# First modulation by column halves with its shift as a one-row product, and the last output block by halves, in an encoder block on one core

## The chip, the core and the metric

The kernel runs on one core of a Trainium2 chip: TensorE (PE) for products, VectorE (DVE) and ScalarE (ACT) for element work, GpSimd (POOL), and SyncE (SP), which issues most transfers. The metric is the device time of one execution in microseconds (us), lower being better; the median of 3 runs is given. One more execution was profiled, and all rows below come from it.

## The reference, cut to what matters

One encoder layer on x (512 tokens by 1024 features, float32) with six modulation vectors of 1024 values:

```
mod = silu(c) @ W_ada + b_ada                 # six pieces of 1024
shift1, scale1, gate1, shift2, scale2, gate2 = split(mod)
h  = rmsnorm(x, g_norm1) * (1 + scale1) + shift1
z  = h @ W_in                                 # q latent 256 | kv latent 128 | rope key 64 | u 512 | v 512
y  = concat(rmsnorm(attention), rmsnorm(gMLP)) @ W_o ;  x = x + gate1 * y
h2 = rmsnorm(x, g_norm2) * (1 + scale2) + shift2
x  = x + gate2 * peer(h2)                     # product-key retrieval over 16384 experts
out = rmsnorm(x, g_final)
```

## The kernel before

Tokens are four blocks of 128 (NB = 4), features eight chunks of 128 (KD = 8). A float32 product of accuracy is three products of split parts (high and low half of each operand): `mm3`, lines 82 to 84; `split_into` makes the parts, the high one on ACT (L77), the low one on DVE (L78).

**The start.** SP loads the first modulation's scale weights (wada, group 1, eight chunks of 128 rows by 1024 columns, 512 KB each), then x (four blocks of 512 KB), then the shift weights (group 0, eight chunks), then the first two weight slabs of the input projection (wl0, wl1). SP's transfers go round over eight lanes, so that each waits for the one eight before it. `mod_cols` forms a modulation vector so: DVE adds up the eight chunks, each scaled by one column of silu(c) (csil), into macc, 128 partitions by 1024 (L143, L149, L146); PE transposes macc in eight pieces (mcol, L159); DVE sums each piece over its columns (L161) and adds the bias (L162). `normed_T` squares the four blocks of x on ACT (sq_n, L183), forms one reciprocal root for all four (n_ms on DVE, L112; n_r on POOL, L114), scales x on DVE (L197), has PE transpose it (trx_n, L201), applies scale and shift (nt_n, "the affine", L189 on DVE, L187 on ACT) and splits the result into hT.

**The projection.** lat (four blocks, 384 columns) and krp (512 columns) are PE products of hT with wl0 and wl1. Then ACT squares lat (sql, sqk), DVE copies it out of PSUM (L320), rq and rkv are formed (L112, L114), DVE scales lat (L326, L327), the rope key is rotated (kr, kr_t, L294 to L296), PE transposes lat (trl, L331), and queries, keys and values follow. kr_sw, which kr_t reads, and the three trl tiles share two PSUM buffers (tag tr).

**Later modulations** (groups 2 to 5) load on POOL's queue, after a marker that POOL copies once the first shift is there (mark, L247), and DVE adds them up between other work. mod_row (L177) multiplies macc by a matrix of ones on PE in two halves of 512 columns, in plain float32.

**The end.** The last four expert tiles' products (held, TAIL = 4) are done block by block of 128 tokens, for each of them the four experts, for each expert both column halves. Then the output blocks (the gather block GB, 0, 1, 2): on DVE times gate2 (L943), plus x (L944); square on ACT (L945); times g_final on DVE (L946); the two sums added (L947); reciprocal root (L112, L114); scaled on ACT in two halves (L951) and stored by SP (L952).

Which instruction of an engine stands where is set by the scheduler of the framework from a model, not by program order; where a stretch is under a manual schedule, its engines keep the program's order.

## Time and profile before

| what | value |
|---|---|
| median of 3 runs | 1567.47 us (1567.18 to 1567.62) |
| profiled execution, its own time | 1570.06 us |
| its span | 1568.3 us |
| mean granted TensorE clock | 0.981 |
| PE, DVE, ACT, POOL busy | 95%, 79%, 41%, 25% of the span |

The profiled execution is 2.59 us above the median; 1.8 us of its time lie outside the span. Times in the rows are microseconds from the span's start. A row of the timeline has the start, the time until its last instruction's end, engine, line, operation, written tile and read tiles, shape, number of instructions, and in brackets how long the engine was idle before it and for whom it waited.

### The profile page before, as it was taken

The numbers are of one execution on the slowest core, as the hardware profiler recorded it, in microseconds if no ns is written. First come the engines' busy times: TensorE is split into PE (matmuls) and PEld (weight loads), VectorE is DVE, ScalarE is ACT, GpSimd is POOL, SyncE is SP. The second block draws the span as 40 slices with busy tenths as digits, with TensorE's granted clock in tenths as the row PEclk, the third lists the DMA queues.
The fourth block names the chain that finished last, engine by engine and source line by source line (L and its number), as shares of the span: only waits on it lengthen the run. The fifth ranks groups of instructions, "written<-read, shape, count | busy, mean of one in ns | idle before, by whom it ended". The sixth has DMA issues, their size and how long they took to land.

```text
span 1568.3 us, 21451 instructions
## 1 busy us (share of the span) xinstructions
PE 1492.6 (95%) x7675; PEld 1317.9 (84%) x7675; DVE 1240.9 (79%) x2388; ACT 636.6 (41%) x1092; POOL 397.1 (25%) x335
## 2 busy tenths in 40 slices
PE   2899999998979999999999999999999999999996
PEld 1765787887879999999999999999999999998884
DVE  6937865579989997987887878878888888886774
ACT  2533434432338997334333333333333333332343
POOL 1202100000000000002554444444544544542210
PEclk9899999999999999999999999999999999999998
DMA  9626334331325769666999999988999998987873
GB/s 366 232 79 223 130 132 148 112 104 48 101 94 159 237 211 300 218 224 220 354 351 319 321 330 328 326 318 318 336 330 314 326 325 315 333 287 230 256 237 121
DMA packets 147226, 380.71 MB, mean 243 GB/s; under 512 B 11184, under 2 KB 59840, under 8 KB 146864
## 3 DMA queue, kind: packets, MB, share of 16 engines
q1 hardware_dynamic: 103472, 221.02, 40.5%
q0 software_dynamic: 42352, 153.62, 28.7%
q10 hardware_dynamic: 1296, 4.72, 0.8%
q8 instruction: 60, 0.98, 0.2%
q14 instruction: 46, 0.38, 0.1%
HBM read 349.16 MB, written 30.15 MB: 242 GB/s over the span
## 4 chain that ended last, share of the span: by engine, by line
PE 86%; DVE 7%; DMA 3%; ACT 1%; issue 1%; POOL 0%; SPq 0%; ACTq 0%; POOLq 0%; DVEq 0%
PE out L83 11%; PE out L84 11%; PE out L82 11%; PE pa L82 11%; PE pa L84 11%; PE pa L83 11%; PE gg L770 5%; DMA wada<-w_ada 2%; PE q L82 1%; PE q L84 1%; PE q L83 1%; PE yo L82 1%; PE yo L84 1%; PE yo L83 1%; DVE macc L149 1%
## 5 line engine op out<-in xcount | busy, mean ns | idle before, releaser
L842 POOL DMA_INDIRECT gu<-peer_u,idx x128 | 181.3, 1417 | 653.6 <-DVE w17l L78 467.6
L842 POOL DMA_INDIRECT gv<-peer_v,idx x128 | 173.0, 1351 | 235.0 <-DVE accg L862 209.0
L850 DVE SCALAR_TENSOR_TENSOR scr<-gu,h2g 128x1024 bf16<-128x1024 f32 x128 | 156.5, 1222 | 24.1 <-DMA gu<-peer_u,idx 21.8
L862 DVE SCALAR_TENSOR_TENSOR accg<-gv,wg,accg 128x1024 f32<-128x1024 f32 x127 | 162.8, 1282 | 7.1 <-DMA gv<-peer_v,idx 4.6
L770 PE MATMUL gg<-o,o 128*128 128x128 f32 x768 | 96.0, 280 | 3.6 <-ACT o L764 2.0
L770 PEld LDWEIGHTS gg<-o,o 128*128 128x128 f32 x768 | 94.6, 196 | 4.1 <-ACT o L764 4.1
L908 DVE TENSOR_TENSOR a<-a,g 128x384 f32<-128x384 f32 x128 | 69.1, 550 | 6.4 <-DMA g<-gd 2.9
L764 ACT ACTIVATE o<-o1b,gT 128x128 f32<-128x128 bf16 x192 | 63.4, 405 | 13.8 <-DVE o1b L751 7.2
L518 ACT ACTIVATE a<-pa 128x384 f32<-128x384 f32 x128 | 61.7, 483 | 13.2 <-PE pa L84 13.2
L149 DVE SCALAR_TENSOR_TENSOR macc<-wada,csil,macc 128x1024 f32<-128x1024 f32 x40 | 51.2, 1280 | 9.5 <-DMA wada<-w_ada 9.1
L753 DVE TENSOR_TENSOR o<-iota_s,gT 128x1024 f32<-128x1024 f32 x48 | 58.4, 1216 | 0.3 <-PE gg L770 0.2
L757 DVE TENSOR_SCALAR o<-iota_s,gT 128x128 f32<-128x128 f32 x192 | 53.2, 339 | 0.0
L779 ACT COPY st<-gg 128x512 f32<-128x512 f32 x96 | 50.5, 581 | 0.0
L159 PE MATMUL mcol<-ident_s,macc 128*128 128x128 f32 x32 | 7.4, 391 | 26.6 <-DVE macc L146 23.1
L135 POOL DMA_DIRECT2D wada<-w_ada x32 | 17.1, 535 | 59.9 <-DVE macc L149 24.3
L159 PEld LDWEIGHTS mcol<-ident_s,macc 128*128 128x128 f32 x32 | 5.5, 201 | 28.3 <-DVE macc L146 17.9
L424 ACT ACTIVATE pe<-s,mx 128x512 f32<-128x512 f32 x16 | 11.0, 688 | 28.4 <-DVE mx L422 20.8
L684 PE MATMUL sc<-keys_s,qT 128*128 128x128 f32 x128 | 18.1, 284 | 2.8 <-ACT qT L681 2.8
L751 DVE TENSOR_TENSOR o1b<-erep,gB 128x512 bf16<-128x512 bf16 x48 | 20.0, 416 | 0.9 <-ACT gB L734 0.9
L684 PEld LDWEIGHTS sc<-keys_s,qT 128*128 128x128 f32 x128 | 15.6, 191 | 5.7 <-ACT qT L681 4.3
L531 DVE MAX8 v12d<-s 128x8 f32<-128x128 f32 x48 | 12.7, 280 | 9.4 <-ACT s L686 9.4
L431 PEld LDWEIGHTS o<-vv,pts 128*128 128x128 f32 x128 | 16.1, 192 | 2.3 <-DVE mx L422 0.8
(2789 smaller groups left out, 4952.2 us busy)
## 6 DMA issues: line engine op xcount, KB each, us to landing
gd<-st SPq DMA_DIRECT2D x12, 1984.0 KB, 7.9
g<-gd SPq DMA_DIRECT2D x31, 768.0 KB, 8.4
wada<-w_ada POOLq DMA_DIRECT2D x32, 512.0 KB, 4.7
wada<-w_ada SPq DMA_DIRECT2D x16, 512.0 KB, 10.1
x<-x SPq DMA_DIRECT2D x4, 512.0 KB, 12.4
x<-x ACTq DMA_DIRECT2D x4, 512.0 KB, 3.8
x2d<-x ACTq DMA_DIRECT2D x4, 512.0 KB, 2.8
gu<-peer_u,idx POOLq DMA_INDIRECT x128, 7.3
```

What stands on the lines that cost most here:

```text
L82: nc.tensor.matmul(o, lhsT=lh, rhs=rh, start=first, stop=False)
L83: nc.tensor.matmul(o, lhsT=lh, rhs=rl, start=False, stop=False)
L84: nc.tensor.matmul(o, lhsT=ll, rhs=rh, start=False, stop=last)
L149: nc.vector.scalar_tensor_tensor(acc, w, csil[:, c:c + 1], acc, op0=ALU.mult, op1=ALU.add)
L518: nc.scalar.activation(t, p[:, :TD], AF.Gelu)
L753: nc.vector.tensor_tensor(o2s[n], iota.unsqueeze(1).to_broadcast([P, UT, P]), tT[:, 1, t0:t0 + UT].unsqueeze(2).to_broadcast([P, UT, P]), ...
L764: nc.scalar.activation(o1s[n][:, i, :], e[:, :, i], AF.Copy, scale=tT[:, 2, t0 + i:t0 + i + 1])
L770: nc.tensor.matmul(pgs[n][i // 4][:, i % 4 * P:(i % 4 + 1) * P], lhsT=o2[:, i, :], rhs=o1[:, i, :], start=True, stop=True)
L842: nc.gpsimd.indirect_dma_start(out=g, out_offset=None, in_=src, in_offset=bass.IndirectOffsetOnAxis(ap=idx[:, s:s + 1], axis=0))
L850: nc.vector.scalar_tensor_tensor(scr, g, 1.0, st["h2g"], op0=ALU.mult, op1=ALU.mult, accum_out=actg[:, n:n + 1])
L862: nc.vector.scalar_tensor_tensor(accg, g, wg[:, s:s + 1], accg, op0=ALU.mult, op1=ALU.add)
L908: nc.vector.tensor_tensor(wv3, wv3, gt[:, :, e % GE, :], op=ALU.mult)
```

## The change

The first modulation's weights are loaded by column halves: each transfer is 256 rows by 512 columns (512 KB), four for a half of scale or shift. SP's order is now scale half 0, x, shift half 0, wl0, scale half 1, shift half 1, wl1, wv0, wv1, wuq, wukv. A scale half is added up on DVE as before, 512 wide (mh), and transposed in four pieces (msc). A shift half is made on PE: eight float32 products of one column of csil with 512 columns of weights, summed in one row of PSUM (msh, 1x512), copied by ACT (mshr), and turned into a column by four products of one column each (mshc); DVE adds the bias. Each block of x gets its own reciprocal root. `hT_half(0)` makes the first four chunks of hT from the first halves, and the second halves follow. The marker waits for the second shift half, and the transfers of perm, of the positions and of group 2 on POOL stand behind it or behind the four reciprocal roots.

At the end PE takes the last block's held products first for column half 0, then for half 1. `output` multiplies only half 0 by g_final ahead of the sum of squares (yg); half 1 is one DVE operation with the root and g_final; half 0 is scaled on ACT and stored by ACT's queue. The output blocks 0, 1 and 2 stand under a manual schedule for DVE and ACT.

```diff
+        def mod_half_load(g, hf):
+            ws = []
+            for k in range(4):
+                w = M0.tile([P, 2, 512], F32, name=f"wada{g}_{hf}_{k}", tag="wada0", bufs=12)
+                nc.sync.dma_start(w, a["w_ada"][k * 256:(k + 1) * 256, g * D + hf * 512:g * D + (hf + 1) * 512]
+                                  .rearrange("(c p) n -> p c n", p=P))
+                ws += [w[:, 0, :], w[:, 1, :]]
+            return ws
+        def scale_half(hf, ws):
+            acc = M0.tile([P, 512], F32, name=f"mh{hf}", tag="mh", bufs=2)
+            nc.vector.tensor_scalar_mul(acc, ws[0], csil[:, 0:1])
+            for c in range(1, KD):
+                nc.vector.scalar_tensor_tensor(acc, ws[c], csil[:, c:c + 1], acc, op0=ALU.mult, op1=ALU.add)
+            p = ps.tile([P, 512], F32, name=f"msc{hf}", tag="mod" if hf else "oacc", bufs=1)
+            for j in range(4):
+                nc.tensor.transpose(p[:, j * P:(j + 1) * P], acc[:, j * P:(j + 1) * P], ident)
+            m = cp.tile([P, 4], F32, name=f"msc_{hf}")
+            nc.vector.reduce_sum(m, p.rearrange("p (j k) -> p j k", k=P), axis=AX.X)
+            nc.vector.tensor_add(m, m, bada[:, KD + hf * 4:KD + hf * 4 + 4])
+            nc.vector.scalar_tensor_tensor(m, m, 1.0, g1c[:, hf * 4:hf * 4 + 4], op0=ALU.add, op1=ALU.mult)
+            return m
+        def shift_half(hf, ws):
+            p = ps.tile([P, 512], F32, name=f"msh{hf}", tag="mod", bufs=1)
+            for c in range(KD):
+                nc.tensor.matmul(p[0:1, :], lhsT=csil[:, c:c + 1], rhs=ws[c], start=c == 0, stop=c == KD - 1)
+            row = M0.tile([1, 512], F32, name=f"mshr{hf}", tag="mshr", bufs=2)
+            nc.scalar.copy(row, p[0:1, :])
+            p = ps.tile([P, 512], F32, name=f"mshc{hf}", tag="mod", bufs=1)
+            for j in range(4):
+                nc.tensor.matmul(p[:, j:j + 1], lhsT=row[:, j * P:(j + 1) * P], rhs=ones[0:1, 0:1],
+                                 start=True, stop=True)
+            m = cp.tile([P, 4], F32, name=f"msh_{hf}")
+            nc.vector.tensor_add(m, p[:, :4], bada[:, hf * 4:hf * 4 + 4])
             return m
...
-        ws1 = [mod_load(1, c) for c in range(KD)]
+        wsc, wsh = [None] * 2, [None] * 2
+        wsc[0] = mod_half_load(1, 0)
         xs = []
         for b in range(NB):
             t = B.tile([P, D], F32, name=f"x{b}", tag=f"y{b}")
             nc.sync.dma_start(t, a["x"][b * P:(b + 1) * P, :])
             xs.append(t)
-        ws0 = [mod_load(0, c) for c in range(KD)]
-        s1 = mod_scale(1, g1c, ws1)
-        sh1 = mod_cols(0, ws0)
+        wsh[0] = mod_half_load(0, 0)
+        s1 = [scale_half(0, wsc[0])]
+        ss1 = cp.tile([P, NB], F32, name="ss1")
+        for b in range(NB):
+            sumsq(xs[b], ss1[:, b:b + 1], f"sq_n{b}")
+            r = rstd_of(ss1[:, b:b + 1], D, f"n{b}")
+            nc.vector.tensor_scalar_mul(xs[b], xs[b], r)
+        sh1 = [shift_half(0, wsh[0])]
+        hT = [B.tile([P, KD, T], F32R, name=f"hT{i}", tag=f"hT{i}") for i in range(2)]
+
+        def hT_half(hf):
+            for j in range(4 * hf, 4 * hf + 4):
+                p = (tr_ps if hf else acc_ps)(f"trx{j}")
+                for b in range(NB):
+                    nc.tensor.transpose(p[:, b * P:(b + 1) * P], xs[b][:, j * P:(j + 1) * P], ident)
+                t = B.tile([P, T], F32, name=f"nt{j}", tag="nt", bufs=2)
+                affine(j, t, p, s1[hf], sh1[hf], j % 4)
+                split_into(hT[0][:, j, :], hT[1][:, j, :], t)
+
+        hT_half(0)
+        wl = load_w("wl", a["w_in"], 0, 512, (0,))
+        wsc[1] = mod_half_load(1, 1)
+        wsh[1] = mod_half_load(0, 1)
+        wl += load_w("wl", a["w_in"], 0, 512, (1,))
+        s1.append(scale_half(1, wsc[1]))
+        sh1.append(shift_half(1, wsh[1]))
         mark = cp.tile([P, 1], F32, name="mark")
-        mark = nc.gpsimd.tensor_copy(mark, sh1[:, 0:1])
-        hT = [B.tile([P, KD, T], F32R, name=f"hT{i}", tag=f"hT{i}") for i in range(2)]
-        normed_T(xs, s1, sh1, hT[0], hT[1], "n1")
+        mark = nc.gpsimd.tensor_copy(mark, sh1[1][:, 0:1])
+        hT_half(1)
...
-            wl = load_w("wl", a["w_in"], 0, 512)
             nc.sync.dma_start(wuq, a["w_uq"].rearrange("(c p) n -> p c n", p=P))
             nc.sync.dma_start(wukv, a["w_ukv"])
...
-                for e_, wh, wl, vh, vl in held:
-                    for hf in range(2):
-                        sl = slice(hf * 512, (hf + 1) * 512)
-                        mm3(outs[2 * b + hf], (wh[:, bs], wl[:, bs]), (vh[:, sl], vl[:, sl]),
-                            e_ == 0, e_ == NE - 1)
+                steps = [(hf, h) for h in held for hf in range(2)]
+                if b == ND - 1:
+                    steps.sort(key=lambda s: s[0])
+                for hf, (e_, wh, wl, vh, vl) in steps:
+                    sl = slice(hf * 512, (hf + 1) * 512)
+                    mm3(outs[2 * b + hf], (wh[:, bs], wl[:, bs]), (vh[:, sl], vl[:, sl]),
+                        e_ == 0, e_ == NE - 1)
             held.clear()
...
-    for b in (GB, 0, 1, 2):
+    halves = [slice(hf * 512, (hf + 1) * 512) for hf in range(2)]
+
+    def output(b):
...
         ss = gp.tile([P, 2], F32, name=f"ssf{b}", tag="ssf", bufs=2)
-        for hf in range(2):
-            sl = slice(hf * 512, (hf + 1) * 512)
+        yg = gp.tile([P, 512], F32, name=f"yg{b}", tag="yg", bufs=2)
+        for hf, sl in enumerate(halves):
             nc.vector.tensor_mul(y[:, sl], accg[:, sl] if b == GB else outs[2 * b + hf], gate2[:, sl])
             nc.vector.tensor_add(y[:, sl], y[:, sl], xr[:, sl])
             nc.scalar.activation(xr[:, sl], y[:, sl], AF.Square, accum_out=ss[:, hf:hf + 1])
-            nc.vector.tensor_mul(y[:, sl], y[:, sl], gfin[:, sl])
+            if hf == 0:
+                nc.vector.tensor_mul(yg, y[:, sl], gfin[:, sl])
         nc.vector.tensor_add(ss[:, 0:1], ss[:, 0:1], ss[:, 1:2])
         r = rstd_of(ss[:, 0:1], D, f"fin{b}")
-        for hf in range(2):
-            sl = slice(hf * 512, (hf + 1) * 512)
-            nc.scalar.activation(y[:, sl], y[:, sl], AF.Copy, scale=r[:, 0:1])
-            nc.sync.dma_start(out[b * P:(b + 1) * P, sl], y[:, sl])
+        nc.scalar.activation(yg, yg, AF.Copy, scale=r[:, 0:1])
+        nc.vector.scalar_tensor_tensor(y[:, halves[1]], y[:, halves[1]], r[:, 0:1], gfin[:, halves[1]],
+                                       op0=ALU.mult, op1=ALU.mult)
+        nc.scalar.dma_start(out[b * P:(b + 1) * P, halves[0]], yg)
+        nc.sync.dma_start(out[b * P:(b + 1) * P, halves[1]], y[:, halves[1]])
+
+    output(GB)
+    with tc.manual_schedule(engines={nc.vector.engine, nc.scalar.engine}):
+        for b in range(ND):
+            output(b)
```

Three places in the orders of the engines, before and after. In the names, a number behind a tile tells one buffer from another.

PE at the start, before: the last transposes of x (x_122 is its fourth block), the shift's transposes (mcol), and the first product of the projection.

```order
L201 MATMUL trx_n_246<-ident_s,x_122 128x128
L201 MATMUL trx_n_255<-ident_s,x_122 128x128
L159 MATMUL mcol_0_176<-ident_s,macc_165 128x128 x4
L159 MATMUL mcol_1_182<-ident_s,macc_165 128x128 x4
L201 MATMUL trx_n_264<-ident_s,x_116 128x128
L201 MATMUL trx_n_264<-ident_s,x_118 128x128
L201 MATMUL trx_n_264<-ident_s,x_120 128x128
L201 MATMUL trx_n_264<-ident_s,x_122 128x128
L82 MATMUL krp<-hT_191,wl0h 128x512
```

PE at the same place after: the first shift half stands between the transposes of the third block of x (x_112) and the fourth (x_114).

```order
L271 MATMUL trx_293<-ident_s,x_112 128x128
L271 MATMUL trx_302<-ident_s,x_112 128x128
L188 MATMUL msh_171<-wada_0_0_116,csil 1x512 x2
L188 MATMUL msh_171<-wada_0_1_118,csil 1x512 x2
L188 MATMUL msh_171<-wada_0_2_120,csil 1x512 x2
L188 MATMUL msh_171<-wada_0_3_122,csil 1x512 x2
L271 MATMUL trx_191<-ident_s,x_114 128x128
...
L271 MATMUL trx_302<-ident_s,x_114 128x128
L193 MATMUL mshc_182<-ones,mshr_180 128x1 x4
L82 MATMUL lat_369<-wl0h,hT_189 128x384
```

The eight transposes of mcol are gone from here, and eight one-row products stand ahead of the fourth block's six transposes. The second halves (four msc, eight msh, four mshc) stand further on in PE's order, between the twelve krp products of wl0 (ten of them come behind msc), after all 48 lat products of wl0.

DVE behind the projection, before, from the last ang step (the rope angles) to the low half of wv1.

```order
L281 TENSOR_SCALAR ang<-ang 128x512
L112 TENSOR_SCALAR rq_ms<-lss 128x4
L320 COPY lat<-lat_337 128x384
L112 TENSOR_SCALAR rkv_ms<-lss 128x4
L326 TENSOR_SCALAR lat<-lat,rq_r 128x256
L327 TENSOR_SCALAR lat<-lat,rkv_r 128x128
...
L327 TENSOR_SCALAR lat<-lat,rkv_r 128x128
L149 SCALAR_TENSOR_TENSOR macc_734<-wada_5_750,csil,macc_734 128x1024
L149 SCALAR_TENSOR_TENSOR macc_734<-wada_6_753,csil,macc_734 128x1024
L295 TENSOR_TENSOR kr<-kr_raw,cos 128x512
L294 TENSOR_TENSOR kr_t<-kr_sw,sin 128x512
L78 TENSOR_TENSOR wv1l<-wv1r,wv1h 128x2048
```

DVE at the same place after.

```order
L355 COPY lat<-lat_372 128x384
L316 SCALAR_TENSOR_TENSOR ang<-rn,ang 128x512
L112 TENSOR_SCALAR rq_ms<-lss 128x4
L112 TENSOR_SCALAR rkv_ms<-lss 128x4
...
L361 TENSOR_SCALAR lat<-lat,rq_r 128x256
...
L362 TENSOR_SCALAR lat<-lat,rkv_r 128x128
...
L362 TENSOR_SCALAR lat<-lat,rkv_r 128x128
L78 TENSOR_TENSOR wv1l<-wv1r,wv1h 128x2048
L331 TENSOR_TENSOR kr<-kr_raw,cos 128x512
L140 SCALAR_TENSOR_TENSOR macc_769<-wada_2_776,csil,macc_769 128x1024
L330 TENSOR_TENSOR kr_t<-kr_sw,sin 128x512
```

rq_ms and rkv_ms stand behind the last copy of lat and an ang step now; wv1l stands ahead of kr and one addition of macc between kr and kr_t, where two additions stood ahead of kr and wv1l behind kr_t. (Two ang steps and the middle scalings of lat are left out.)

DVE at the end, before: the output blocks (yf_13590 is block 0, yf_13611 block 1, yf_13632 block 2) are interleaved.

```order
L943 TENSOR_TENSOR yf_13611<-out_5445,gate_84 128x512
L946 TENSOR_TENSOR yf_13590<-yf_13590,gfin 128x512 x2
L947 TENSOR_TENSOR ssf_13591<-ssf_13591 128x1
L944 TENSOR_TENSOR yf_13611<-yf_13611,xr_13609 128x512
L112 TENSOR_SCALAR fin_ms<-ssf_13591 128x1
L943 TENSOR_TENSOR yf_13611<-out_5446,gate_84 128x512
L946 TENSOR_TENSOR yf_13611<-yf_13611,gfin 128x512
L944 TENSOR_TENSOR yf_13611<-yf_13611,xr_13609 128x512
L943 TENSOR_TENSOR yf_13632<-out_5447,gate_84 128x512
L943 TENSOR_TENSOR yf_13632<-out_5448,gate_84 128x512
L946 TENSOR_TENSOR yf_13611<-yf_13611,gfin 128x512
```

DVE at the end after (yf_13627 is block 0, yf_13648 block 1).

```order
L983 TENSOR_TENSOR yf_13627<-yf_13627,xr_13625 128x512
L987 TENSOR_TENSOR ssf_13628<-ssf_13628 128x1
L112 TENSOR_SCALAR fin_ms<-ssf_13628 128x1
L990 SCALAR_TENSOR_TENSOR yf_13627<-yf_13627,fin_r,gfin 128x512
L982 TENSOR_TENSOR yf_13648<-out_5480,gate_84 128x512
L983 TENSOR_TENSOR yf_13648<-yf_13648,xr_13646 128x512
L986 TENSOR_TENSOR yg_13650<-yf_13648,gfin 128x512
L982 TENSOR_TENSOR yf_13648<-out_5481,gate_84 128x512
L983 TENSOR_TENSOR yf_13648<-yf_13648,xr_13646 128x512
L987 TENSOR_TENSOR ssf_13649<-ssf_13649 128x1
L112 TENSOR_SCALAR fin_ms<-ssf_13649 128x1
```

Block 1 begins after block 0's last operation, which reads the root (fin_r); block 2 stands behind block 1 in the same way.

## Rows read from the trace of the kernel before

**Rows 1.** The profile page: the chain of work that ended last, by engine, as shares of the span; and a line of the transfers (tile, queue, number, KB each, median us from issue to landing).

```profile
PE 86%; DVE 7%; DMA 3%; ACT 1%; issue 1%; POOL 0%; SPq 0%; ACTq 0%; POOLq 0%; DVEq 0%
...
wada<-w_ada POOLq DMA_DIRECT2D x32, 512.0 KB, 4.7
```

**Rows 2.** The chain that ended last, in order of time: start, length, engine, tile, line and number of instructions merged.

```profile
22.07 1.16 ACT sq_n L183 x2
23.58 1.04 POOL n_r L114
...
40.16 2.28 DVE wl0l L78
43.09 0.79 PE krp L83
...
116.89 0.86 PE mrow L177 x2
```

**Rows 3.** The timeline of DVE at the start (chunks of the scale weights, scaling of x, first affine), then of ACT (squares of x, first and last block).

```profile
10.10 1.28 DVE L149 SCALAR_TENSOR_TENSOR macc<-wada,csil,macc 128x1024 f32<-128x1024 f32 x1 [0.19 <-DMA wada<-w_ada]
11.58 1.29 DVE L149 SCALAR_TENSOR_TENSOR macc<-wada,csil,macc 128x1024 f32<-128x1024 f32 x1 [0.20 <-DMA wada<-w_ada]
13.14 1.28 DVE L149 SCALAR_TENSOR_TENSOR macc<-wada,csil,macc 128x1024 f32<-128x1024 f32 x1 [0.27 <-DMA wada<-w_ada]
15.80 1.28 DVE L149 SCALAR_TENSOR_TENSOR macc<-wada,csil,macc 128x1024 f32<-128x1024 f32 x1 [1.38 <-DMA wada<-w_ada]
17.12 1.41 DVE L146 SCALAR_TENSOR_TENSOR macc<-wada,csil,macc 128x512 f32<-128x512 f32 x2
...
24.64 0.75 DVE L197 TENSOR_SCALAR x<-x,n_r 128x1024 f32<-128x1024 f32 x1 [1.22 <-POOL n_r L114]
...
39.43 0.81 DVE L189 TENSOR_SCALAR nt_n<-trx_n,mcolb,mcolb 128x512 f32<-128x512 f32 x1
...
18.26 1.06 ACT L183 ACTIVATE sq_n<-x 128x1024 bf16<-128x1024 f32 x1 [15.49 <-DMA x<-x]
...
22.07 1.06 ACT L183 ACTIVATE sq_n<-x 128x1024 bf16<-128x1024 f32 x1 [0.15 <-DMA x<-x]
```

**Rows 4.** The timeline of PE: transposes of x, the last product of lat, and transposes of 128 by 128 later in the kernel (pt).

```profile
25.45 2.87 PE L201 MATMUL trx_n<-ident_s,x 128*128 128x128 f32 x12 [5.56 <-DVE x L197]
28.64 1.34 PE L201 MATMUL trx_n<-ident_s,x 128*128 128x128 f32 x6 [0.32 <-DVE x L197]
30.49 0.88 PE L201 MATMUL trx_n<-ident_s,x 128*128 128x128 f32 x6 [0.52 <-DVE x L197]
...
63.92 0.34 PE L84 MATMUL lat<-wl1h,hT 128*128 128x384 f32 x1
...
166.69 0.60 PE L427 MATMUL pt<-ident_s,pe 128*128 128x128 f32 x4
```

**Rows 5.** Busy time of the engines in stretches: the stretch, its length, then for PE, PEld, DVE, ACT and POOL the busy time (and instructions), the granted TensorE clock as a share of full speed, the DMA share and GB/s.

```profile
33.50:34.00 0.50, 0.00 (x0) 0.00 (x0) 0.50 (x1) 0.00 (x0) 0.00 (x0) 0.50 1.05 410
...
43.10:46.40 3.30, 3.30 (x9) 2.82 (x10) 3.30 (x3) 2.63 (x4) 0.00 (x0) 0.50 0.99 376
46.70:50.00 3.30, 3.30 (x19) 3.07 (x18) 3.12 (x6) 1.92 (x3) 0.55 (x1) 1.00 1.04 389
...
78.00:98.00 20.00, 20.00 (x54) 9.78 (x53) 10.89 (x15) 8.00 (x14) 1.50 (x3) 1.00 0.30 109
```

**Rows 6.** The timeline behind the projection: DVE, and the transposes of lat on PE.

```profile
63.30 0.68 DVE L280 SCALAR_TENSOR_TENSOR ang<-rn,ang 128x512 f32<-128x512 f32 x1
...
64.86 0.17 DVE L112 TENSOR_SCALAR rq_ms<-lss 128x4 f32<-128x4 f32 x1
65.26 0.56 DVE L320 COPY lat<-lat 128x384 f32<-128x384 f32 x1 [0.23 <-ACT sqk L183]
...
68.74 2.60 DVE L149 SCALAR_TENSOR_TENSOR macc<-wada,csil,macc 128x1024 f32<-128x1024 f32 x2
71.26 0.68 DVE L295 TENSOR_TENSOR kr<-kr_raw,cos 128x512 f32<-128x512 f32 x1
71.86 0.68 DVE L294 TENSOR_TENSOR kr_t<-kr_sw,sin 128x512 f32<-128x512 f32 x1
...
72.60 1.76 PE L331 MATMUL trl<-ident_s,lat 128*128 128x128 f32 x7 [1.63 <-DVE kr_t L294]
```

**Rows 7.** The timeline of two DVE operations of 128 by 512 of which the second reads the first's result.

```profile
224.86 0.68 DVE L487 TENSOR_TENSOR yg<-yo,gate 128x512 f32<-128x512 f32 x1
225.57 0.69 DVE L488 TENSOR_TENSOR x<-x,yg 128x512 f32<-128x512 f32 x1
```

**Rows 8.** The timeline of the end: the last product on PE, DVE's first operation of block 0 and the sum of squares of block 2, and ACT of block 2 (its last square, and the scaling that waits for the root).

```profile
1552.95 0.40 PE L84 MATMUL out<-v127h,w127l 128*128 128x512 f32 x1
...
1545.76 1.29 DVE L943 TENSOR_TENSOR yf<-out,gate 128x512 f32<-128x512 f32 x2 [0.96 <-PE out L84]
...
1559.03 0.15 DVE L947 TENSOR_TENSOR ssf<-ssf 128x1 f32<-128x1 f32 x1
...
1557.68 0.61 ACT L945 ACTIVATE xr<-yf 128x512 f32<-128x512 f32 x1
1558.20 0.19 ACT L945 ACTIVATION_READ_ACCUMULATOR xr<-yf 128x1 f32 x1
1560.10 1.33 ACT L951 ACTIVATE yf<-yf,fin_r 128x512 f32<-128x512 f32 x2 [1.71 <-POOL fin_r L114]
```

More of the change, by code (lines that the diff above doesn't have):

```diff
@@ L183, in sumsq, with affine, load_w @@
             nc.scalar.activation(sq[:, :w], src, AF.Square, accum_out=dst)
[L185 removed]
+        def affine(j, t, p, scol, shcol, c=None):
+            sl = slice(j, j + 1) if c is None else slice(c, c + 1)
             if j % 2:
[L187 removed]
+                nc.scalar.activation(t, p, AF.Identity, scale=scol[:, sl], bias=shcol[:, sl])
             else:
[L189 to L208 removed]
+                nc.vector.tensor_scalar(t, p, scol[:, sl], shcol[:, sl], op0=ALU.mult, op1=ALU.add)
+        def load_w(name, src, c0, w, khs=(0, 1)):
             res = []
[L210 removed]
+            for kh in khs:
                 raw = B.tile([P, 4, 512], F32, name=f"{name}{kh}r", tag="wr", bufs=2)
```

49 lines of the change are left out of this document (10 added, 39 removed).

## The prediction, made before the changed kernel ran

> **What bounds the kernel now.** I read the chain of waits first. PE holds 86% of it, DVE 7% and transfers 3% [rows 1], so time can be won only where PE is not yet, or no longer, the bound: at the two ends. The chain in order of time and the DVE and ACT timelines tell the start. The last block of x is squared at 22.07, because x is queued behind all eight scale chunks; root, scaling of x and the eight additions of the shift follow on DVE, and the first affine starts at 39.43; the first product that waits for its split starts at 43.09, with the weight split of 2.28 between them [rows 2, 3]. PE then works until the last lat product at 63.92 [rows 4], which ends in effect at 64.1. Behind it DVE's kr_t lets trl start at 72.60 [rows 6]. From 78 to 98 PE is busy for all of 20.00 us [rows 5]: a shift of trl passes one for one into the rest. At the end PE's last product starts at 1552.95, and the last scaling on ACT ends at 1560.10 + 1.33 = 1561.43 [rows 8]. So I add three terms: last lat product, lat to trl, and tail.
>
> **Start, up to the first affine.** What goes: eight shift additions and sixteen transposes. Transfers keep their size and count, so the landing pace stays: chunks 4 to 7 were waited for at 10.10, 11.58, 13.14 and 15.80, and the eighth was there by 17.12 [rows 3]. With four transfers of scale ahead, x takes the places from 11.6 to 17.1, and the first shift half those where x stood, 18.3 to 22.1 [rows 3]. The third block of x: landed at 15.8, squared and read in 1.16, then from the end of that to its transposes 25.45 - 23.23 = 2.2 before, of which 1.04 is the root for four columns [rows 2, 4]; for one column it was about half a microsecond less in the end's chain (sum to scaling 1.07 in all [rows 8]). So its six transposes start at 18.9 and end 1.34 later [rows 4], at 20.3.
>
> There PE meets the first shift half, ahead of the fourth block. Its price is the unknown. The nearest row is mrow, a plain float32 product with 512 moving columns: 0.86 at the upper level [rows 2], hence 1.72 at the lower. The row written is one partition instead of 128; bounds for one product are 0.43 (half the passes) and 1.72 (lower level throughout). I take 0.86, since the moving columns are the same. The level itself: in the stretch from 43.10 the granted clock was 0.50 (1.2 GHz) under dense products until 46.40, and 1.00 (2.4 GHz) from 46.70 on; at 33.50, with PE idle since 31.4, it was 0.50 [rows 4, 5]. Six transposes took 1.34 from 28.64 and 0.88 from 30.49 [rows 4], so it rose under transposes alone, some 4 us after they began at 25.45. Now eighteen transposes stand between 15 and 20.3 with a gap of a microsecond, and the rise falls between 20.3 and 23.7. I take 22.0: one product at 1.72, seven at 0.86, end at 28.0.
>
> The Trainium skill, page "TensorE: Matmul & The Clock Gate", section "Part 4: PE-mode transpose", says that such transposes don't count as PE work for the clock. The pair 1.34 and 0.88 [rows 4] speaks against it here. By that rule the rise would come as far into the shift products as it came into the products from 43.10 on, two of them would be at the lower level, and the sum below would be 0.9 more.
>
> After 28.0: the fourth block's transposes 0.9 [rows 4], with ACT's copy beside them; four one-column products, not shown by any row, between four times 0.11 (the step of the pt transposes [rows 4]) and 1.5, taken at 0.9; DVE's addition 0.3. The first affine is at 30.1 instead of 39.43, 9.3 earlier.
>
> **From there to the last lat product.** Before, 64.1 - 39.43 = 24.7, with the clock low for the first 3.3 us of products; PE idles as long ahead of them now, so that stays. Added on PE: eight products of the second shift half, 6.9; four scale transposes 0.45; four one-column products 0.8; together 8.1. None of this is hidden: PE has no gap between the first products and the last lat, and from 46.70 to 50.00 is busy for all 3.30 [rows 5]. Before, these sums lay on DVE, whose time there was spent anyhow. And there is a second start: affine to product is 43.09 - 39.43 = 3.7 [rows 2, 3], again with a weight split (wv0l, 2.28 as wl0l) ahead of hT's; two krp products and eight transposes, 1.4, are all that PE has left for that time, so 2.3 idle. Sum 10.4: the last lat product ends at 30.1 + 24.7 + 10.4 = 65.2. **Term 1: +1.1.** The second halves' transfers follow wl0 at the old pace and land before 36, with their readers later: no cost.
>
> **From lat to trl.** rq_ms stood at 64.86; now it is behind the last copy (65.26 + 0.56) and an ang step of 0.6 [rows 6]: 66.4, +1.6. Roots and scalings are as before. Then wv1l, 2.2, stands ahead of kr in place of two additions, 2.5; and an addition, 1.2, between kr and kr_t [rows 6]: +0.9. trl waits for kr_t as before, since the buffers are the same. **Term 2: +2.5**, on top of term 1.
>
> **Modulation groups and other queues, at nothing.** POOL's transfers of group 2 wait for the marker some 15 us longer; their additions slide behind the projection, where DVE is busy 10.89 of 20 [rows 5]; their reader is mrow at 116.89 [rows 2]. If that cover were gone, up to six additions of 1.28, 7.7, would show. The first addition stands in DVE's order ahead of two hT splits, about 6 us behind the loads' issue; they take 4.7 to land [rows 1]; a later landing stops the splits, and PE behind them, one for one. On SP's queue, wv1 waits for wl1's buffer, and wuq and wukv wait behind it: 10 us of cover. For the gather block, one scaling on ACT ahead of a weight cast: at most 0.5.
>
> **Tail.** PE's sort brings block 2's first half 2.8 us (twelve products) forward, but DVE is not there. The manual schedule makes each block wait for its own root. A block on DVE: multiply, add, yg, multiply, add, with steps of 0.71 where one reads the other [rows 7] and 0.61 where not [rows 8]: the second add ends at 2.74 + 0.68 = 3.4; hand-over 0.1 and square with its read 0.7 [rows 8]: 4.2; from the sum to the scaling 1.07 [rows 8]: 5.3; the last operation 0.7, the next block starting at 6.0. Block 0 starts at 1545.76 [rows 8] as before, block 2 at 1557.7, its last operation ends at 1563.7, against 1561.43. **Term 3: +2.3** (1.8 to 3). The stores are the same size; ACT's copy of the other half ends at the same time.
>
> **Sum:** 1.1 + 2.5 + 2.3 = +5.9: 1576.0 against the profiled 1570.06, and 1573.4 on the median 1567.47, which lies 2.59 lower; a stretch at either end doesn't scale with that.
>
> **Rivals.**
> - *The one-row products leave the clock low.* Only one column of the array works. Then the first half costs 8 x 1.72, 6.0 more; the second lets the clock fall half-way, 3.4 more, and lat starts again at half speed, 1.7 more: +17.0, 1584.5. Against it: transposes alone raised it.
> - *The clock is up when the shift starts, and stays up.* Shift 0.9 less, and no lower level at lat, 1.6 less: +3.4, 1570.9. For it: transposes raised it; against: PE idles some 4 us ahead of lat, and such a stretch had ended at 0.50 [rows 5].
> - *The other side: a one-row product costs 0.43.* 3.5 less at the first half, 3.4 at the second: -1.0, 1566.5, not slower. It decides from a price of 0.67 down. Against it: mrow's 0.86 for the same columns.
> - *The tail does what the halves are for,* the three blocks overlapping on DVE: block 2's last operation would follow the last product (1553.35) by 5 us, 1558.4, 3.0 earlier than before: +0.6, 1568.1. Against it: DVE's order has the root's reader ahead of the next block.
>
> **How the numbers follow.** About 0.2%, 3.1 us, can be told from no change. Forecast 0.53; low clock 0.12; clock up 0.17; half price 0.08; overlapping tail 0.06; none of these 0.04. Slower: nearly all of the forecast, the low clock and two thirds of the clock-up case: 0.76. Same: what is left of these, most of the half-price and tail cases: 0.18. Faster: 0.06, half price together with a milder term. The range leaves out half price, part of the tail case and the far part of the low clock: 1568.3 to 1583.0.
>
> **What would show it.** In the changed profile: x squared from about 11.6; shift products 0.86 apart from 22 on, first affine at 30; last lat product near 65, trl near 76; at the end DVE idle before each root's reader, blocks 6.0 apart, the last operation ending 2.3 later against the span's start, plus the shift of terms 1 and 2. It would be wrong if the first affine came at 28 or 36 (price or clock), if PE had slack where I see none, or if the tail's blocks overlapped.

## The result, and the profile after

The changed kernel takes 1577.08 us (median of 6 runs, 1575.74 to 1580.37), the kernel before 1567.55 (6 runs, 1567.01 to 1569.22). The ratio is 1.0061, with a 95% interval of 1.0048 to 1.0074: slower by 9.5 us, where 5.9 were forecast; the time lies inside the range given. The profiled execution of the changed kernel took 1576.77 with a span of 1575.0. Between the two profiled executions the spans differ by only 6.7, since before's lay 2.5 above its median. Executions of one kernel differ by some 3 us, the longer ones mostly at the lower mean granted clock (of 24 of the kernel before, taken beside the last experiments, those at 0.981 to 0.983 took 1569.0 to 1571.0, the others 1565.2 to 1568.3, and before's profiled one had 0.981), so I read sums from landmarks inside a span and verdicts from medians.

The landmarks, in us from the span's start:

| | first affine | second start's first affine | last lat product | trl, second group | DVE starts block 0 | last operation ends | span |
|---|---|---|---|---|---|---|---|
| before | 39.43 | – | 63.92 | 72.60 | 1545.76 | 1561.43 | 1568.3 |
| forecast | 30.1 | – | +1.1 | +3.6 | – | +2.3 after the shift | – |
| after | 29.00 | 53.56 | 66.78 (+2.9) | 78.25 (+5.7) | 1549.48 | 1567.56 | 1575.0 |

PE's timeline of the changed kernel, from the first transposes of x to trl:

```profile
15.65 4.38 PE L271 MATMUL trx<-ident_s,x 128*128 128x128 f32 x18 [2.35 <-DVE x L263]
19.96 7.03 PE L188 MATMUL msh<-wada,csil 128*1 128x512 f32 x16
26.92 0.87 PE L271 MATMUL trx<-ident_s,x 128*128 128x128 f32 x6
27.74 1.02 PE L193 MATMUL mshc<-ones,mshr 1*128 1x1 f32 x8
...
44.19 7.03 PE L188 MATMUL msh<-wada,csil 128*1 128x512 f32 x16
...
53.59 0.40 PE L84 MATMUL krp<-hT,wl0l 128*128 128x512 f32 x1
56.26 0.44 PE L82 MATMUL lat<-wl1h,hT 128*128 128x384 f32 x1 [1.17 <-ACT hT L77]
...
58.07 0.52 PE L83 MATMUL lat<-wl1l,hT 128*128 128x384 f32 x1
58.39 0.52 PE L82 MATMUL lat<-wl1h,hT 128*128 128x384 f32 x1
...
66.78 0.33 PE L84 MATMUL lat<-wl1h,hT 128*128 128x384 f32 x1
...
78.25 1.97 PE L366 MATMUL trl<-ident_s,lat 128*128 128x128 f32 x8 [1.50 <-DVE kr_t L330]
```

Each shift product is two records; sixteen in 7.03 are 0.88 a product, the price of mrow [rows 2], although its row has one partition. The first eight start at 19.96 and run at that price from the first, so the first affine comes at 29.00, 1.1 earlier than forecast: the clock's rise, forecast for 22.0, stands in this trace's clock records at 19.7, just ahead of the first product. The other eight stand from 44.19 to 51.2 without a gap. Then PE has six krp products, the four one-column products and transposes of x left and waits until 56.26, and at 58.07 the lat products are 0.32 apart instead of 0.17 as at the upper level. The granted clock tells why. Windows of the same kernel (busy time and count of PE, PEld, DVE, ACT, POOL, then the granted clock, the DMA share and GB/s):

```profile
20.00:27.00 7.00, 7.00 (x18) 1.30 (x18) 0.12 (x1) 0.00 (x0) 0.24 (x1) 1.00 1.05 384
...
31.00:34.50 3.50, 2.99 (x9) 2.25 (x9) 3.50 (x5) 1.54 (x3) 0.00 (x0) 0.50 1.05 387
...
57.40:60.60 3.20, 3.20 (x12) 3.10 (x11) 3.20 (x5) 1.39 (x3) 0.00 (x0) 0.50 1.01 374
```

The clock is at its upper level (2.4 GHz) under the first shift and at the lower (1.2 GHz) at the first start, as before [rows 5], but for longer: the lat products stay 0.32 apart until 36.5, so that some sixteen products fall into it, against ten in before, which is some 0.6 more by my estimate. It falls a second time, from 57.2 to 60.65; the nine products in that stretch cost some 1.4 more than at the upper level (eight lat products 0.15 each, one krp product 0.20).

DVE's and ACT's timelines of the changed kernel, through the second start and behind the projection:

```profile
53.56 0.81 DVE L219 TENSOR_SCALAR nt<-trx,msc,msh 128x512 f32<-128x512 f32 x1
55.72 2.29 DVE L78 TENSOR_TENSOR wv0l<-wv0r,wv0h 128x2048 fp32r<-128x2048 f32 x1 [1.35 <-ACT wv0h L77]
57.93 1.29 DVE L78 TENSOR_TENSOR hT<-nt,hT 128x512 fp32r<-128x512 f32 x2
...
69.19 0.16 DVE L112 TENSOR_SCALAR rq_ms<-lss 128x4 f32<-128x4 f32 x1
73.52 2.28 DVE L78 TENSOR_TENSOR wv1l<-wv1r,wv1h 128x2048 fp32r<-128x2048 f32 x1
75.72 0.68 DVE L331 TENSOR_TENSOR kr<-kr_raw,cos 128x512 f32<-128x512 f32 x1
76.32 1.27 DVE L140 SCALAR_TENSOR_TENSOR macc<-wada,csil,macc 128x1024 f32<-128x1024 f32 x1
77.52 0.68 DVE L330 TENSOR_TENSOR kr_t<-kr_sw,sin 128x512 f32<-128x512 f32 x1
```

```profile
53.79 1.90 ACT L77 CAST wv0h<-wv0r 128x2048 fp32r<-128x2048 f32 x1 [1.96 <-PE krp L83]
55.59 0.61 ACT L77 CAST hT<-nt 128x512 fp32r<-128x512 f32 x1
```

At the second start ACT casts a slab of the value weights (wv0h, 1.90) ahead of the first block of hT, and DVE splits it (2.29) ahead of hT's low part; the values are needed long after. Behind the projection the second slab's split and an addition of group 2 stand ahead of kr_t, for which trl waits, as forecast from [rows 6].

The tail, DVE's timeline of the changed kernel, and then the issue of its last two stores:

```profile
1549.48 0.69 DVE L982 TENSOR_TENSOR yf<-out,gate 128x512 f32<-128x512 f32 x1 [1.03 <-PE out L84]
...
1554.81 0.75 DVE L990 SCALAR_TENSOR_TENSOR yf<-yf,fin_r,gfin 128x512 f32<-128x512 f32 x1 [0.73 <-POOL fin_r L114]
1555.48 0.68 DVE L982 TENSOR_TENSOR yf<-out,gate 128x512 f32<-128x512 f32 x1
...
1566.81 0.75 DVE L990 SCALAR_TENSOR_TENSOR yf<-yf,fin_r,gfin 128x512 f32<-128x512 f32 x1 [0.73 <-POOL fin_r L114]
```

```profile
1567.56 0.37 ACTq L992 DMA_DIRECT2D out_dram<-yg  x1
1567.58 0.33 SPq L993 DMA_DIRECT2D out_dram<-yf  x1
```

Blocks start 6.00 apart (1549.48, 1555.48) with DVE idle ahead of each root's reader. From block 0's start to the last operation's end it takes 18.1, before 15.67 [rows 8]: +2.4.

**The sum** of the span's 6.7: last lat product +2.9; lat to trl +2.8; 1.0 regained by the first qn product (80.3 before, 84.9 after); 0.9 more regained on the way to the last product (1552.95 before, 1556.71 after); tail +2.4; and 0.6 behind the last operation. The regained parts count against the others; the rounded terms add up to 6.8.

Where the 1.0 came from, three traces tell. Below are the rows from trl on and a window around the clock's level, first in before, then in the changed kernel, then in the kernel before with the new tail alone (the second experiment), which has the same start as before:

```profile
78.47 1.10 PE L292 MATMUL qr_sw<-qr_raw,perm_s 128*128 128x512 f32 x2
70.90:77.70 6.80, 5.17 (x14) 3.21 (x14) 5.64 (x6) 2.06 (x3) 1.41 (x4) 0.52 0.69 205
```

```profile
83.15 1.11 PE L328 MATMUL qr_sw<-qr_raw,perm_s 128*128 128x512 f32 x2
74.30:81.10 6.80, 5.30 (x16) 3.26 (x16) 6.80 (x7) 2.06 (x3) 1.12 (x2) 0.50 0.61 206
```

```profile
72.36 1.09 PE L331 MATMUL trl<-ident_s,lat 128*128 128x128 f32 x8 [1.75 <-DVE kr_t L294]
...
75.87 1.11 PE L292 MATMUL qr_sw<-qr_raw,perm_s 128*128 128x512 f32 x2
72.40:78.40 6.00, 6.00 (x20) 2.90 (x20) 5.86 (x6) 2.38 (x4) 1.62 (x3) 1.00 0.72 251
```

From trl to the first qr_sw it is 5.87 in before (72.60 to 78.47, clock 0.52), 4.90 in the changed kernel (78.25 to 83.15, clock 0.50 for its first part) and 3.51 in the tail alone (72.36 to 75.87, clock 1.00). So the 1.0 is no slack on PE: the profiled execution of before lost 2.4 there to a fall of the clock ahead of trl, and the changed kernel 1.4. Not every execution of one start has that fall, and before's 2.4 are of the size of the 2.5 by which it lay above its median. The later 0.9 was not traced to its place.

### The profile page after: what moved, and what is told of

Same layout as the page of the kernel before. It is cut to its first block, busy times and chain, and to the rows that moved or that the text cites. A ratio compares the mean times of both kernels' runs of the same rounds, so it can differ in the third digit from the quotient of the medians.

```text
span 1575.0 us, 21538 instructions
## 1 busy us (share of the span) xinstructions
PE 1508.1 (96%) x7715; PEld 1319.8 (84%) x7715; DVE 1233.9 (78%) x2390; ACT 635.3 (40%) x1090; POOL 398.2 (25%) x338
## 4 chain that ended last, share of the span: by engine, by line
PE 86%; DVE 8%; DMA 2%; ACT 1%; issue 1%; POOL 0%; SPq 0%; POOLq 0%; DVEq 0%; ACTq 0%
PE out L84 11%; PE out L83 11%; PE out L82 11%; PE pa L82 11%; PE pa L84 11%; PE pa L83 11%; PE gg L805 5%; DMA wada<-w_ada 2%; PE q L82 1%; PE q L84 1%; PE q L83 1%; PE yo L82 1%; PE yo L84 1%; PE yo L83 1%; PE msh L188 1%
## 5 line engine op out<-in xcount | busy, mean ns | idle before, releaser
L140 DVE SCALAR_TENSOR_TENSOR macc<-wada,csil,macc 128x1024 f32<-128x1024 f32 x28 | 35.9, 1280 | 7.3 <-DMA wada<-w_ada 6.9
L453 PE MATMUL s<-kr,qr 64*128 64x512 f32 x32 | 18.0, 641 | 0.0
L114 POOL TENSOR_TENSOR n_r<-n_ms,nhalf 128x1 f32<-128x1 f32 x8 | 4.8, 600 | 50.9 <-DVE n_ms L112 42.9
```

## Experiments

**Theory A**: the sixteen shift products lie on PE's path, and what the start wins is spent on them. **Theory B**: the products are paid for by the earlier start, and what costs is the second start and the order around it: weight casts ahead of hT, the clock's second fall, wv1l and additions ahead of kr_t. For the tail: the manual schedule serialises the blocks, against a cost of the halves themselves.

**The start alone.** The changed kernel with the old output loop and the old order of the held products:

```diff
-    with tc.manual_schedule(engines={nc.vector.engine, nc.scalar.engine}):
-        for b in range(ND):
-            output(b)
+    for b in (GB, 0, 1, 2):          # loop as before
...
-                if b == ND - 1:
-                    steps.sort(key=lambda s: s[0])
```

> The changed kernel with the end of the kernel before (no sort of the last block's products, no manual schedule, output blocks as before); the start stays changed. Theory (the tail's blocks wait one by one for their own roots, and that costs 2.4 whatever the start does): 2.4 to 3.0 below the changed kernel, so about 7 above the kernel before, near 1574.5. Rival (the changed tail costs nothing by itself, and its later end only passes the start's loss on): as the changed kernel, near 1577.

Measured: 1573.6, ratio 1.0044 [1.0030, 1.0058] (here and below against the kernel before, timed beside the run). Last lat product at 66.14, trl at 77.63, and the tail took 15.7 from 1546.35 to 1562.05, as in before. The start alone makes the kernel slower; against the whole change it saves 0.17%, 2.7 us, which is the tail's share.

**The tail alone**, on the kernel before:

```diff
-    for b in (GB, 0, 1, 2):          # loop of before
+    output(GB)
+    with tc.manual_schedule(engines={nc.vector.engine, nc.scalar.engine}):
+        for b in range(ND):
+            output(b)
...
+                if b == ND - 1:
+                    steps.sort(key=lambda s: s[0])
```

> The kernel before with the changed end alone (sort, halves, manual schedule). Theory: DVE's last operation ends 2.4 later, blocks 6.0 apart; 2.4 to 3.0 above the kernel before, near 1570.3. Rival (the changed tail is neutral or gains on its own, and the loss lies in the start alone): at or below 1567.5.

Measured: 1571.2, ratio 1.0025 [1.0015, 1.0035]; 18.1 from block 0's start (1543.91) to the last operation's end (1561.99). The tail alone costs 0.25%.

**The same tail, in the scheduler's own order:**

```diff
-    with tc.manual_schedule(engines={nc.vector.engine, nc.scalar.engine}):
-        for b in range(ND):
-            output(b)
+    for b in range(ND):
+        output(b)
```

> The kernel before with the changed end, but without the manual schedule, so that the scheduler interleaves the output blocks on DVE and ACT. Theory (the manual order, not the halves, is what costs): DVE's operations, 14 steps of 0.61 with one root's reader of 0.65 up to block 2's second addition, then about 3.2 of square, root and last operation; the last one ends near 1558.8 instead of ACT's 1561.4, so 2 to 3 below the kernel before, near 1565. Rival (the halves themselves cost, by the extra DVE operation with the root or the store on ACT's queue): 1 or more above the kernel before.

Measured: 1566.85, ratio 0.9995 [0.9986, 1.0004]. DVE's timeline of this kernel, first and last operation of the tail:

```profile
1545.28 1.29 DVE L947 TENSOR_TENSOR yf<-out,gate 128x512 f32<-128x512 f32 x2 [1.02 <-PE out L84]
...
1558.11 0.75 DVE L955 SCALAR_TENSOR_TENSOR yf<-yf,fin_r,gfin 128x512 f32<-128x512 f32 x1 [0.72 <-POOL fin_r L114]
```

DVE now takes both halves of block 0 at once, and the last operation ends 13.58 behind block 0's start: 4.5 less than under the manual schedule. So the schedule is the cause. My 2 to 3 us below before were not reached in the median. The chain is 2.1 shorter than before's 15.67, but 0.6 of it goes behind the last operation: span end less last operation is 7.44 here, 7.41 in the tail alone and 7.44 in the changed kernel, against 6.87 in before and 6.85 in the start alone. The two last stores leave together, and out_dram's rows give 2.6 at the least and 2.8 in the median from issue to landing in the changed kernel, where the start alone, with stores one behind the other, has 2.0 and 2.1. The rest of the missing gain, some 1.4 us, is of the size of the interval.

**The shift on DVE instead of PE**, with the old tail, so that no product is left on PE:

```diff
-            for c in range(KD):
-                nc.tensor.matmul(p[0:1, :], lhsT=csil[:, c:c + 1], rhs=ws[c], ...)
+            nc.vector.tensor_scalar_mul(acc, ws[0], csil[:, 0:1])
+            for c in range(1, KD):
+                nc.vector.scalar_tensor_tensor(acc, ws[c], csil[:, c:c + 1], acc, ...)
+            # then four transposes and a sum over columns, as scale_half does
```

> As e1_old_tail, but both shift halves are added up on DVE and transposed, as the scale halves are, in place of the one-row products on PE. Theory (the one-row products lie on the path, 7 at the second half and some 4 at the first affine): first affine near 25 instead of 29, last lat product near 58 instead of 67; against e1_old_tail 8 less, near 1566.5, and so level with or below the kernel before. Rival (what costs is the second start of the projection and the order behind it, and DVE becomes the bound with the additions back on it): last lat product not before 64, 3 or less below e1_old_tail.

Measured: 1578.22, ratio 1.0074 [1.0060, 1.0088]. My expectation fell: this is 4.6 slower than the start alone. DVE's and PE's rows of this kernel:

```profile
58.73 0.75 DVE L138 TENSOR_SCALAR macc<-wada,csil 128x1024 f32<-128x1024 f32 x1 [4.95 <-DMA wada<-w_ada]
```

```profile
60.14 0.69 PE L84 MATMUL lat<-wl1h,hT 128*128 128x384 f32 x1 [4.55 <-DVE hT L78]
```

The first addition of group 2 stood ahead of hT's low parts in DVE's order, and its transfer landed late: DVE waited 4.95 and PE behind it 4.55. This is the stop that the prediction named as a risk of the changed kernel; it did not happen there and did here. The run says nothing against A, since it put another wait in the products' place.

**Cheaper products.** ACT casts the shift's weights and csil to the single-pass form; the low parts are left out:

```diff
+        csr = cp.tile([P, KD], F32R, name="csr")
+        nc.scalar.copy(csr, csil)
...
+                w = M0.tile([P, 2, 512], F32R, ...)
+                nc.scalar.copy(w, wt[k])
-                nc.tensor.matmul(p[0:1, :], lhsT=csil[:, c:c + 1], rhs=ws[c], ...)
+                nc.tensor.matmul(p[0:1, :], lhsT=csr[:, c:c + 1], rhs=wr[c], ...)
```

> As e1_old_tail, but the one-row products run on the high parts alone: ACT casts the shift's weights and csil to float32r, and each product is one pass; the low parts of these operands are left out. Theory A (the products' 0.86 apiece lie on the path at both halves): products at 0.22, first affine near 25.5 instead of 28.5, last lat product 5 to 8 earlier than e1_old_tail's 66.3, time 5 to 7 below e1_old_tail, near 1567.5. Theory B (the second start of the projection sets the end: what DVE and ACT must do between the second shift half and the first lat product of wl1, at a low clock): first affine earlier as well, but the last lat product not before 64 and 2.5 or less below e1_old_tail.

Measured: 1563.45, ratio 0.9965 [0.9952, 0.9978]. PE's timeline of this kernel:

```profile
41.41 2.01 PE L200 MATMUL msh<-wshr,csr 128*1 128x512 f32 x8
...
57.79 0.33 PE L84 MATMUL lat<-wl1h,hT 128*128 128x384 f32 x1
```

Eight products take 2.01 instead of 7.03. Against the start alone the first affine comes 3.6 earlier, the last lat product 8.35 earlier, and the ratio falls from 1.0044 to 0.9965, some 12 us, with intervals of about 2 us either way on each. With 10.0 us less of products on PE, 8.35 came back at lat, where the order at the second start is the same as in the start alone: A holds, the products are on the path nearly one for one.

**Casts and additions behind hT**, products as in the change, old tail:

```diff
+        hT_done = (last_hi[0], last_lo[0])       # hT's last cast and split
+        with tc.issue_after(hT_done[0].ins), tc.issue_after(hT_done[1].ins):
+            wv = load_w("wv", a["w_in"], 1024, 512)
-        with tc.issue_after(mark.ins):
+        with tc.issue_after(mark.ins), tc.issue_after(hT_done[1].ins):
             mod_row(2, gate1)
```

> As e1_old_tail, but the casts and low halves of wv and the additions of group 2 are made to stand behind the second half's hT on ACT and DVE; products as in e1_old_tail. Theory A: PE's work ahead of the last lat product is the same, so the last lat product moves by 1 at most (66.3), and the time with it, near 1573. Theory B: the 1.9 of wv0h and 2.3 of wv0l no longer stand ahead of hT, PE idles less and its clock falls less; the last lat product comes 2 to 4 earlier, time 2 to 4 below e1_old_tail, near 1570.5.

Measured: 1573.08, ratio 1.0032 [1.0022, 1.0042]. The granted clock of this kernel at the second start, in a window:

```profile
54.00:57.50 3.50, 2.96 (x18) 2.28 (x17) 2.78 (x4) 2.50 (x4) 2.80 (x6) 1.00 0.75 185
```

PE's pause before lat is shorter and the clock stays up. The last lat product comes at 64.44 instead of 66.14, although the first affine was 0.8 later here: the second start's order costs 1.7 to 2.5 in the change. But trl comes 12.4 behind lat, as the casts now stand there, and the ratio moved by only 0.12%, with intervals that overlap. So B is part of the cause at lat, and gives little unless the order behind lat is mended too.

**Both: sums on DVE and that order** (the shift on DVE, as in the run of that name, together with the order of the run just above):

> As e8_order, with both shift halves on DVE as in e4_shift_dve. In that run the first lat products of wl1 waited 4.55 for hT's low half, because an addition of group 2 stood ahead of it on DVE and waited 4.95 for its weights. Theory A: without that wait the additions on DVE cost less than the products on PE: last lat product near 60, time 4 to 6 below e1_old_tail. Theory B (DVE is the bound when the additions are on it, the second affine not before 50.5 in either place): last lat product near 62 to 63, about level with e8_order.

Measured: 1569.5, ratio 1.0008 [0.9999, 1.0017]; last lat product at 62.97, trl at 74.19. With the stop gone, and with the same order in both, the sums on DVE are 1.5 better at lat than the products on PE (62.97 for 64.44), far less than the 14.1 that the products take. DVE, which has scale, roots and affines there too, becomes the bound ahead of the second halves of hT. DVE's and PE's rows of this kernel there:

```profile
47.11 2.28 DVE L79 TENSOR_TENSOR wl1l<-wl1r,wl1h 128x2048 fp32r<-128x2048 f32 x1
...
50.10 0.16 DVE L210 TENSOR_TENSOR msh<-msh,bada_s 128x4 f32<-128x4 f32 x1
50.30 0.81 DVE L233 TENSOR_SCALAR nt<-trx,msc,msh 128x512 f32<-128x512 f32 x1
```

```profile
51.22 1.97 PE L285 MATMUL trx<-ident_s,x 128*128 128x128 f32 x8 [3.25 <-ACT nt L231]
```

The shift's last sum stands behind a weight split in DVE's order, the second start's first affine behind that sum, and PE waits 3.25.

**The order behind lat.** The start alone, with the value weights and group 2 behind the rope key:

```diff
-                nc.scalar.copy(raw, p)
+                ri = nc.scalar.copy(raw, p)
-                nc.vector.tensor_mul(t, sw, sin)
+                ti = nc.vector.tensor_mul(t, sw, sin)
+                kr_done.append((ri, ti))
+        with tc.issue_after(kr_done[0][0].ins), tc.issue_after(kr_done[0][1].ins):
+            wv = load_w("wv", a["w_in"], 1024, 512)
+        with tc.issue_after(mark.ins), tc.issue_after(kr_done[0][1].ins):
             mod_row(2, gate1)
```

> As e8_order, but wv's casts and low halves and the additions of group 2 stand behind the rotated rope key (kr_raw on ACT, kr_t on DVE), so nothing of them is between the last lat product and trl. Both theories: the second start as in e8_order. Term 2 of the prediction (2.5 from DVE's order behind the projection): trl's second group starts 6 to 7 behind the last lat product instead of 11.3, so 4 to 5 below e8_order, near 1566.5 and so level with the kernel before. If the order on DVE is not what delays trl (roots on POOL or kr_raw on ACT end last instead): less than 2 below e8_order.

Measured: 1565.5, ratio 0.9984 [0.9975, 0.9993], 0.6% below the start alone. DVE's and PE's rows of this kernel:

```profile
65.03 0.17 DVE L113 TENSOR_SCALAR rq_ms<-lss 128x4 f32<-128x4 f32 x1 [0.23 <-ACT sql L213]
69.72 0.68 DVE L333 TENSOR_TENSOR kr<-kr_raw,cos 128x512 f32<-128x512 f32 x1
70.33 0.68 DVE L331 TENSOR_TENSOR kr_t<-kr_sw,sin 128x512 f32<-128x512 f32 x1
```

```profile
71.06 1.09 PE L368 MATMUL trl<-ident_s,lat 128*128 128x128 f32 x8 [1.07 <-DVE kr_t L331]
```

From the last lat product (64.09) to trl it is 7.0, against 11.5 in the changed kernel and 8.7 in before. The four rows answer to [rows 6]: rq_ms is again 0.94 behind lat, and no weight split and no addition of group 2 stands ahead of kr or kr_t. The edit moves the value weights' casts on ACT as well: kr_raw's copy there starts 3.2 behind the last lat product here (67.28) and 6.65 behind it in the changed kernel (73.43). So term 2 is an order on DVE and ACT, not work that has to be there; the share of each engine was not tried. Part of the gain is the clock: the granted clock here is 1.00 from 71.00 to 77.00, behind trl, where the changed kernel had 0.50 from 74.30 to 81.10.

**Is it the start that wins, then?** The same order on the kernel before, nothing else changed:

> The kernel before with e13_kr_first's order alone (wv's casts and low halves and the additions of group 2 behind the rotated rope key); start and end as before. Theory (the order behind the projection is a gain of its own, and the changed start as such is worth nothing): last lat product at 64 as before, trl's second group 7 behind it, at 71.1 instead of 72.6; time 1 to 2 below the kernel before and level with e13_kr_first. Rival (the changed start is worth something once that order is mended): e13_kr_first 2 or more below this run.

Measured: 1565.43, ratio 0.9985 [0.9976, 0.9993]. PE's row of this kernel:

```profile
70.95 1.09 PE L333 MATMUL trl<-ident_s,lat 128*128 128x128 f32 x8 [1.07 <-DVE kr_t L295]
```

The last lat product stands at 63.97, and trl starts level with that of the changed start (70.95 and 71.06); the medians are level too. In one order, no difference from the start by column halves is seen, with intervals of 0.1% either way: its ten us at the first affine are all spent before lat.

**The best of it.** With that order, the sums on DVE:

> As e13_kr_first, with both shift halves on DVE. From e9_dve_order (last lat product at 63.0) and e13_kr_first (trl 7 behind it): trl's second group at 70, 1 earlier than e13_kr_first, time 0.5 to 2 below it, near 1564.5. If the additions on DVE hold up what stands behind the projection: at or above e13_kr_first.

Measured: 1563.86, ratio 0.9974 [0.9965, 0.9983]; last lat product at 62.23, trl at 69.20.

And a mixed shift, four chunks added up on DVE, four products on PE and one more for the sum, with the tail in the scheduler's order:

```diff
+            for c in range(1, 4):
+                nc.vector.scalar_tensor_tensor(acc, ws[c], csil[:, c:c + 1], acc, ...)
+            for c in range(4, KD):
+                nc.tensor.matmul(p[0:1, :], lhsT=csil[:, c:c + 1], rhs=ws[c], start=c == 4, stop=False)
+            nc.tensor.matmul(p[0:1, :], lhsT=ones[:, 0:1], rhs=acc, start=False, stop=True)
```

> As e13_kr_first, but each shift half is shared: DVE adds up its first four chunks, PE multiplies the other four and then DVE's sum (by a column of ones), five products instead of eight; and the end as in e3_tail_free. Theory (each one-row product taken off PE gives back its 0.86, as long as DVE has room): first affine near 27, last lat product 4 to 5 earlier than e13_kr_first, near 59.5, trl near 66.5; with some 1.5 at the end, 5 to 7 below e13_kr_first, near 1560. Rival (DVE is the bound there, as with all eight on it): last lat product not before 62, and no more than 3 below e13_kr_first.

Measured: 1562.89, ratio 0.9969 [0.9958, 0.9981]; last lat product at 62.31, where 59.5 was expected, trl at 69.62; the rival named with that expectation, little gain at lat, is what came. It is the fastest kernel here that computes the whole, 0.3% below before, but its interval overlaps the last one's: that the mixed shift is better than DVE's is not shown, and it has the other tail as well.

## Why the prediction was right, point by point

The sign, the range and the three places were right. Term 1, the moment of the clock's rise, and what follows the last operation were mis-sized, and the total came nearer than its parts: term 1 was off by 1.8 rather than 2.9 because the earlier rise gave 1.1 back, which was luck.

- **The price of the one-row product** was right: 0.88 measured for 0.86 taken. Half price, the rival on the other side, is ruled out by the rows from 19.96 and 44.19.
- **The clock under the first shift**: the reading of [rows 4], a rise under transposes alone, was right, and its moment was wrong. The rise came at 19.7 instead of 22.0, so no product ran at the lower level; that gave 0.7 of the 1.1 at the first affine, and the rest came from an earlier start (19.96 for 20.3). That a rise can also fail to come under the transposes, the tail alone shows, which has the start of before:

```profile
28.49 1.54 PE L201 MATMUL trx_n<-ident_s,x 128*128 128x128 f32 x6 [0.32 <-DVE x L197]
30.35 1.54 PE L201 MATMUL trx_n<-ident_s,x 128*128 128x128 f32 x6 [0.32 <-DVE x L197]
...
43.55 0.63 PE L84 MATMUL krp<-hT,wl0l 128*128 128x512 f32 x1
43.98 0.63 PE L82 MATMUL krp<-hT,wl0h 128*128 128x512 f32 x1
...
42.90:44.40 1.50, 1.44 (x3) 1.16 (x4) 1.50 (x4) 1.50 (x2) 0.00 (x0) 1.00 1.05 421
```

  There both groups of six transposes take 1.54, the krp products are 0.43 apart, as at the lower level, and the first rise on record is at 44.7. The window's 1.00 ahead of it is no reading of the level: the clock records of a trace begin with the first rise, and the view prints 1.00 until then. The rival "up and stays up" was right as to the shift and wrong behind it: 0.50 in the stretch from 31.00, and again from 57.40.
- **Term 1** was mis-sized: +2.9 for +1.1; from the first affine to the end of the last lat product it took 38.0 for the 35.1 of the forecast. The products were sized rightly, as the one-pass run shows (8.35 back at lat). The second start was not: it was taken at 2.3 us of idle time and one weight split, and its order held a second weight, wv0, ahead of hT on ACT and DVE, and the clock fell again. The run with the casts behind hT gives 1.7 to 2.5 for both together. That the fall goes with the pause is seen in the nine traces of a changed start: it is there in seven, each with a pause of PE ahead of the second lat products or their transposes (1.17 in the changed kernel), and not in the two that have none as long (casts behind hT, rope key first); what share each has was not tried. The longer low stretch at the first start makes some 0.6 more. With the order mended (the rope key first) the stretch took 35.2 (first affine 29.10, last lat product 64.09), but without the split of wv0, which the 35.1 had.
- **Term 2** was right: +2.8 for +2.5 (rq_ms +1.5 for 1.6, the rest +1.3 for 0.9). Its cause, the order ahead of kr_t, is shown by the run with the rope key first, on DVE and ACT together, where the prediction named DVE alone.
- **Groups and queues at nothing** held in the changed kernel, where the first addition stopped nobody; with the sums on DVE it stopped PE for 4.55.
- **A shift of trl passes one for one into the rest**: not in these two executions, where 1.9 of 5.7 was regained by the last product. 1.0 of it is the clock behind trl, which cost before's profiled execution more, and no slack on PE; where the other 0.9 lies stays open.
- **Term 3** was right for its chain (+2.4 for +2.3, blocks 6.0 apart), and its cause, the manual schedule, is shown by taking it away. It lacked the 0.6 of two stores that leave together.

With the sizes measured the span's sum is 6.7 in place of 5.9, and before's 2.5 above its median, the size of its fall of the clock ahead of trl, make most of the rest to 9.5.

## What to carry to other kernels

Ten us won at the first affine came to nothing, since work went from an engine with time to spare at the start to the one that is the bound from there on; ask what the bound's engine has to do in all up to the point where the paths meet, not when its first input comes. Here, cutting a start in two bought a second start, with its own pause, its own fall of the clock and its own order of casts. Look through the order for work that is needed late and stands ahead of what the bound waits for: moving the value weights and one modulation behind the rope key gave, on the kernel before, as much as the whole changed start with that order (ratios 0.9985 and 0.9984).

## What the runs showed of the hardware that was not expected

- A plain float32 product of one stationary column costs as much as one of 128 for 512 moving columns: 0.88. In the single-pass form it is 0.25 (8 in 2.01).
- TensorE's clock rose to its upper level while PE had done nothing but transposes: in all nine traces of the changed start the first rise on record is at 18.9 to 20.8, ahead of the first product, and in three of the four with the old start at 28.4 to 29.6. In the fourth, the tail alone, it is at 44.7, behind the first products. The Trainium skill, page "TensorE: Matmul & The Clock Gate", section "Part 4: PE-mode transpose", has transposes not count as PE work for the clock; these traces speak against it, as the prediction held.
- Two stores of 256 KB issued at once on two queues landed 2.6 at the least after their issue; one behind the other on SP's queue, 2.0.
